# An RWKV/HGRN mixer layer: blockwise transposes by way of DRAM, and a planner's clock for SyncE's queue

## The chip, the cores and the metric

One core of a Trainium2 chip runs the kernel. The metric is the device time of one execution in microseconds; the time before is the median of three runs. Engines are named as the profile names them: PE (TensorE matmul), PEld (its weight loads), DVE (VectorE), ACT (ScalarE), POOL (GpSimd), SP (SyncE, which here only issues DMAs).

## The reference, cut to what matters

One layer over 512 frames and 2048 channels: one input projection, two groups of heads, one output projection, a LayerNorm.

```python
proj = einsum('btd,dc->btc', h, w_in)                 # 512 x 2048 x 8320
rw   = token_shift(proj[..., :RWKV_COLS], shift_mu)   # r, k, v, z and the two low ranks
o    = rwkv7_scan(r, decay, k, v, -kk, kk * a)        # 16 heads of 64, S: 64 x 64 each
o    = (o - mu) * rsqrt(var + GN_EPS) * gn_w + gn_b   # per head
o    = o + sum(r * k * r_k) * v
o_rwkv = o * silu(z)
o_hgrn = rmsnorm(hgrn2_chunkwise(q, f, k, i)) * g_norm_w * silu(z_h)   # 8 heads of 128
y    = einsum('btc,cd->btd', concat([o_rwkv, o_hgrn]), w_out)
out  = layer_norm(ALPHA * x + y, ln_w, ln_b)
```

## The kernel before

**Main stream.** All projections are float32 made of three fp32r products (high x high, high x low, low x high), by the helper `three`; this is PE's main stream, 3900 matmuls. Weights come as `wr` tiles of 512 KB over SP's queue (two buffers); ACT makes the high part `wh` of each half, DVE the low part `wl` (three buffers each). The input projection runs unit by unit in the order of `_order()`. The output projection comes last, in four quarters of 512 columns. A quarter of the first kind has 16 steps of 12 matmuls; a step takes one 128-channel tile of the gated result, split into `xh` (ACT) and `xl` (DVE), against one weight part `wh`, `wl`. At the start of each step `ahead` has the tile of the next step split and reloads tiles that were spilled; in step 8 of the first quarter (steps count from 0) it also sends the DMA of the LayerNorm weights, `big<-ln_wb`, 2 MB. The last four steps use HGRN head 6, RWKV pair 6, HGRN head 7 and RWKV pair 7.

**Side work.** RWKV's 16 heads go as 8 pairs of 128 channels, two pairs to a group. `rwkv_prep` makes a pair's chunked operands: `ar` and `bk` (beta and k times the inverse decay, 8 chunks of 128 columns), scores, and `zz`, which holds v transposed. `rwkv_invert` inverts the chunks' triangular matrices, `rwkv_scan` goes through 8 chunks for two pairs in step, `outputs` adds the part within chunks, and `rwkv_finish` normalizes a pair's result (frames on partitions), turns it back to channels on partitions and gates it.

**The planner.** All engines run in the order in which the Python code issues instructions. `Plan` holds a clock for each engine and a ready and a busy time for each tile, by fixed costs. After every main matmul `pump` goes through queues of generators and issues what its clocks take to be ready: PE work no earlier than 0.35 us after its operands (`LEAD`), other engines' work when it can start within 0.6 us, or its operands come within 0.5 us. `fetched` gives the ready time of a loaded tile: a DMA clock, 360 GB/s and 2 us.

**Transposes before.** `turned` transposes `bk` and v in 32 x 32 blocks on DVE (`dtr`) and then moves the blocks with DMAs from SBUF to SBUF, 32 KB each in runs of 128 bytes: 16 for `bk`, 8 for v. `rwkv_finish` turns its result on PE instead: four `tr` into one PSUM bank, read from there by DVE.

Of the kernel before, what the change touches and what calls it, by code (L numbers as in the profile page):

```python
# [7 lines left out]
F32 = mybir.dt.float32  # L8
# [54 lines left out]
class Plan:  # L63
# [15 lines left out]
    def __init__(self, room):  # L79
        self.clock = {"pe": 0.0, "dve": 0.0, "act": 0.0, "pool": 0.0, "dma": 0.0}  # L80
# [161 lines left out]
def mixer_kernel(ctx, tc, head, x_r, w_all, par, up, ln_wb, consts, hmask, out):  # L242
# [64 lines left out]


# [83 lines left out]
    def turned(dst, src, tmp, rows=4, base=0):  # L392


        name = dst.tensor.name
        yield dtr(tmp, src)
        yield lambda: by_now(tmp)
        for a in range(4):
            for b in range(rows):
                o = base + 32 * b  # L400
                nc.sync.dma_start(dst[o : o + 32, :, 32 * a : 32 * a + 32],
                                  tmp[32 * a : 32 * a + 32, :, 32 * b : 32 * b + 32])
            at = plan.clock["pe"] + 0.4 * rows
            yield lambda: plan.clock["pe"] >= at
        plan.ready[name] = (plan.clock["pe"] + 3.0, "dma")
# [21 lines left out]
    def load(j):  # L427
        if j < nload:
            raws[j] = st("wr", [P, HALF])
            nc.sync.dma_start(raws[j], w_all[j - nhead])  # L430
            plan.fetched(raws[j], 4 * HALF)
# [116 lines left out]
    def constants():  # L548
        raw = st("ksq", [P, T])[:, : 16 * len(LEVELS)]
        for t, a in ((pr, par), (cst, consts), (raw, hmask)):  # L550
            nc.sync.dma_start(t, a)
# [48 lines left out]
    def put_gated(k, g):  # L600

        gated[k] = g
        if k in SPILL:
            def run():
                yield lambda: by_now(g)
                nc.sync.dma_start(spill[SPILL.index(k)], g)
# [8 lines left out]
    def next_up():  # L615
        if len(ups) < NPAIR:
            upw = take("up", [P, 2, P])
            nc.sync.dma_start(upw, up[len(ups)])
# [3 lines left out]
    hc = [slice(64 * h, 64 * h + 64) for h in range(2)]  # L622

    def rwkv_prep(S, p):
# [98 lines left out]
        yield from turned(bk, bk, tmp)  # L723
        drop(tmp)
# [15 lines left out]
        z = take("zz", [P, NCH, P])  # L740
        yield room(ksq=1)
        tmp = take("ksq")
        yield from turned(z, chunks(v), chunks(tmp), rows=2, base=64)
# [3 lines left out]
    def from_v(SS, sc):  # L747
# [6 lines left out]
        for half, (z, ps) in enumerate(zip(zs, pss)):  # L754
            for c in range(NCH):
                for h in range(2):
                    yield mm(ps[hc[h], c * C : c * C + C], sc[64:128, 0, half * 16 + 2 * c + h],
                             z[64:128, c, hc[h]])

        def keep():  # L760
            for z, ps in zip(zs, pss):
                for h in range(2):
                    yield copy(z[0:64, :, hc[h]], chunks(ps[hc[h]]))
# [4 lines left out]
    def outputs(SS, sc):  # L768
# [3 lines left out]
        for half, (S, po) in enumerate(zip(SS, pss)):  # L772
            z = S["zz"]
            yield lambda z=z: by_now(z)
            for c in range(0, NCH, 2):
                for h in range(2):
                    for e in range(2):
                        yield mm(po[hc[e], c // 2 * P + 64 * h : c // 2 * P + 64 * h + 64],
                                 sc[:, 1, half * 16 + 2 * (c + e) + h], z[:, c + e, hc[h]])
# [52 lines left out]
    def rwkv_scan(SS, sc):  # L832
# [11 lines left out]

        for rt, bds, o in zip(rts, bdss, os):
# [5 lines left out]
        for c in range(NCH):  # L851
            more = c < NCH - 1
            zs = [zz[:, c] for zz in zzs]
            news = [bds[c % 2] for bds in bdss]
            pxs = []
            if c > 0:
# [5 lines left out]
                for rt, px, z in zip(rts, pxs, zs):  # L862
                    yield stt(rt[0:64], px[0:64, :P], -1.0, z[0:64], ALU.mult, ALU.subtract)
# [803 lines left out]
```

## Time and profile before

| | |
|---|---|
| Runs | 1050.54 us median of 3 (1049.99 to 1050.96) |
| The profiled execution | 1050.24 us; span 1048.5 us, granted TensorE clock 0.999 |
| DVE, ACT busy | 72% and 42% of the span |
| DMA packets | 87305, of these 56368 under 512 bytes |
| `q<-q` and `zz<-ksq` (blocks moved by `turned`) | 128 and 64 issues of 32 KB |
| Output projection | from 849.7 us on |

The page gives busy times and, in its fourth part, the chain of work that ended last; the timeline gives the start of each instruction, from which PE's real pace is read, since the recorded durations of its matmuls overlap.

### The profile page before, as it was taken

The numbers are of one execution on the slowest core, as the hardware profiler recorded it, in microseconds if no ns is written. First come the engines' busy times: TensorE is split into PE (matmuls) and PEld (weight loads), VectorE is DVE, ScalarE is ACT, GpSimd is POOL, SyncE is SP. The second block draws the span as 40 slices with busy tenths as digits, with TensorE's granted clock in tenths as the row PEclk, the third lists the DMA queues.
The fourth block names the chain that finished last, engine by engine and source line by source line (L and its number), as shares of the span: only waits on it lengthen the run. The fifth ranks groups of instructions, "written<-read, shape, count | busy, mean of one in ns | idle before, by whom it ended". The sixth has DMA issues, their size and how long they took to land.

```text
span 1048.5 us, 18840 instructions
## 1 busy us (share of the span) xinstructions
PE 1040.6 (99%) x7342; PEld 865.1 (83%) x7342; DVE 755.7 (72%) x1653; ACT 437.6 (42%) x867; POOL 38.3 (4%) x81
## 2 busy tenths in 40 slices
PE   9999999999999999999999999999999999999997
PEld 8888888888888888888888888888888888888885
DVE  7465898667759987676689866865998778625556
ACT  6545333445353354452533353525334554323321
POOL 0000000000000000000000000000000002000000
PEclk9999999999999999999999999999999999999999
DMA  8134342222343522223534323234352244545613
GB/s 332 54 103 114 99 109 86 86 79 81 84 123 100 122 82 74 78 98 79 138 78 118 98 62 96 70 96 110 100 128 72 69 164 131 182 131 159 202 60 131
DMA packets 87305, 114.79 MB, mean 109 GB/s; under 512 B 56368, under 2 KB 58160, under 8 KB 87088
## 3 DMA queue, kind: packets, MB, share of 16 engines
q1 hardware_dynamic: 87072, 113.39, 36.6%
q8 instruction: 58, 0.95, 0.4%
q14 instruction: 31, 0.25, 0.1%
q10 hardware_dynamic: 144, 0.20, 0.1%
HBM read 99.92 MB, written 7.34 MB: 102 GB/s over the span
## 4 chain that ended last, share of the span: by engine, by line
PE 99%; DVE 1%; DVEq 0%; issue 0%
PE main L453 74%; PE mix L324 11%; PE mix L453 8%; PE main L1192 3%; PE main L324 2%; PE mix L328 1%; PE mix L1142 0%; DVE inv L356 0%; DVE inv L347 0%; DVE stats L1549 0%; DVEq L1663 0%; DVE mv L1357 0%; DVE bd L356 0%; DVE mv L352 0%; DVE inv L1140 0%
## 5 line engine op out<-in xcount | busy, mean ns | idle before, releaser
L453 PE MATMUL main<-xl,wh 128*128 128x512 f32 x864 | 341.1, 395 | 0.0
L453 PE MATMUL main<-xh,wl 128*128 128x512 f32 x864 | 341.1, 395 | 0.0
L453 PE MATMUL main<-xh,wh 128*128 128x512 f32 x864 | 340.9, 395 | 0.0
L337 ACT ACTIVATE wh<-wr 128x512 fp32r<-128x512 f32 x299 | 186.9, 627 | 237.1 <-PE main L453 180.5
L347 DVE TENSOR_TENSOR wl<-wr,wh 128x512 fp32r<-128x512 f32 x299 | 203.8, 682 | 61.8 <-ACT wh L337 60.1
L453 PEld LDWEIGHTS main<-xh,wh 128*128 128x128 f32 x864 | 162.4, 188 | 33.0
L453 PEld LDWEIGHTS main<-xh,wl 128*128 128x128 f32 x864 | 162.5, 188 | 32.6
L453 PEld LDWEIGHTS main<-xl,wh 128*128 128x128 f32 x864 | 162.4, 188 | 32.6
L453 PE MATMUL main<-wl,xh 128*128 128x512 f32 (+1 forms) x262 | 102.6, 392 | 0.0
L453 PE MATMUL main<-wh,xh 128*128 128x512 f32 (+1 forms) x262 | 102.1, 390 | 0.0
L453 PE MATMUL main<-wh,xl 128*128 128x512 f32 (+1 forms) x262 | 101.6, 388 | 0.0
L453 PEld LDWEIGHTS main<-wh,xh 128*128 128x128 f32 x262 | 49.2, 188 | 9.9
L453 PEld LDWEIGHTS main<-wh,xl 128*128 128x128 f32 x262 | 49.2, 188 | 9.7
L453 PEld LDWEIGHTS main<-wl,xh 128*128 128x128 f32 x262 | 49.2, 188 | 9.6
L338 ACT ACTIVATE t<-main,om 128x512 f32<-128x512 f32 x33 | 22.4, 687 | 51.1 <-PE main L453 41.6
L356 DVE SCALAR_TENSOR_TENSOR t<-main,pr,t 128x511 f32<-128x511 f32 x33 | 24.4, 747 | 26.5 <-ACT t L338 26.2
L347 DVE TENSOR_TENSOR inv<-inv,inv 64x30 f32<-64x30 f32 (+14 forms) x120 | 38.6, 322 | 2.9
L347 DVE TENSOR_TENSOR inv<-inv 64x30 f32<-64x30 f32 (+14 forms) x120 | 38.4, 320 | 2.3
L347 DVE TENSOR_TENSOR t<-t,tot 128x256 f32<-128x256 f32 x96 | 37.8, 414 | 1.8 <-PE mix L324 1.7
L356 DVE SCALAR_TENSOR_TENSOR bd<-mix,pc,bd 64x64 f32<-64x64 f32 x112 | 31.7, 283 | 7.5 <-PE mix L324 5.2
L337 ACT ACTIVATE zz<-mix 64x64 f32<-64x64 f32 x63 | 13.8, 220 | 46.9 <-PE mix L324 45.8
L338 ACT ACTIVATE t<-main 128x512 f32<-128x512 f32 x32 | 18.5, 598 | 30.7 <-PE main L453 30.2
(222 smaller groups left out, 1328.0 us busy)
## 6 DMA issues: line engine op xcount, KB each, us to landing
wr<-w_all SPq DMA_DIRECT2D x156, 512.0 KB, 3.6
q<-head SPq DMA_DIRECT2D x15, 448.0 KB, 5.9
q<-q SPq DMA_DIRECT2D x128, 32.0 KB, 2.4
g<-x_r SPq DMA_DIRECT2D x16, 256.0 KB, 3.8
spill<-g SPq DMA_DIRECT2D x12, 256.0 KB, 2.7
out<-q SPq DMA_DIRECT2D x12, 256.0 KB, 2.4
t<-spill SPq DMA_DIRECT2D x10, 256.0 KB, 4.2
zz<-ksq SPq DMA_DIRECT2D x64, 32.0 KB, 2.6
```

The source lines that it names most:

```text
L324: return Op([("pe", cost, lambda: pe.matmul(o, l, r, start=start, stop=stop, **kw))], [l, r], [o], mode="narrow" if narrow else "main" if ...
L328: return Op([("pe", 0.11, lambda: pe.transpose(o, i, ident))], [i], [o])
L337: return "act", cost, lambda: sc_e.activation(o, i, f, scale=scale)
L338: return "act", cost, lambda: sc_e.activation(o, i, f, scale=scale, bias=bias)
L347: return dve_op([a, b], o, lambda: dve.tensor_tensor(o, a, b, f), base=0.16 if o.shape[0] < P and size(o) == C and o.tensor.name in tags e ...
L356: return dve_op([a, b], o, lambda: dve.scalar_tensor_tensor(o, a, s, b, f1, f2), per=0.00113, base=0.085 if o.shape[0] == P else 0.25 if s ...
L453: pe.matmul(ps, l, r, start=first and i == 0, stop=last and i == 2)
L1192: pe.matmul(pss[a], *ops, start=k == 0 and low == of == 0, stop=k == KT - 1 and low == 1)
```

## The change

`turned` now sends the result of the block transpose to DRAM in one DMA (`far`, 1024 or 512 columns for each partition) and reads it back in one DMA for each 32 rows of the result (four for `bk`, two for v, four for a pair's end), in runs of 1 KB or 512 bytes. The result stands by blocks of 32 columns; for `bk` ACT copies it into the order of chunks, in a `q4` tile that takes `bk`'s place; `zz` keeps the order of blocks, and its readers index it so. `rwkv_finish` turns its normalized result by the same way in place of the four PE transposes; ACT then applies the scale and the bias, and two products on DVE follow. A group's two ends have a queue each. `send` issues every DMA of SP and moves a new clock of the planner, 0.44 us an issue; the ready times of loads start from it, with 1.8 us in place of 2.

```diff
@@ Plan
-        self.clock["dma"] = max(self.clock["dma"], self.clock["pe"]) + size * 128 / 360e3
-        self.ready[tile.tensor.name] = (self.clock["dma"] + 2.0, "dma")
+        self.clock["dma"] = max(self.clock["dma"], self.clock["sp"]) + size * 128 / 360e3
+        self.ready[tile.tensor.name] = (self.clock["dma"] + 1.8, "dma")
@@ helpers
+    def send(o, i):
+        nc.sync.dma_start(o, i)
+        plan.clock["sp"] = max(plan.clock["sp"], plan.clock["pe"]) + 0.44
-    def turned(dst, src, tmp, rows=4, base=0):
-        name = dst.tensor.name
-        yield dtr(tmp, src)
-        yield lambda: by_now(tmp)
-        for a in range(4):
-            for b in range(rows):
-                o = base + 32 * b
-                nc.sync.dma_start(dst[o : o + 32, :, 32 * a : 32 * a + 32],
-                                  tmp[32 * a : 32 * a + 32, :, 32 * b : 32 * b + 32])
-            at = plan.clock["pe"] + 0.4 * rows
-            yield lambda: plan.clock["pe"] >= at
-        plan.ready[name] = (plan.clock["pe"] + 3.0, "dma")
+    def turned(dst, src, tmp, base=0):
+        c = src.shape[1]
+        n = src.shape[2] // 32
+        yield dtr(tmp, src.rearrange("p c (b f) -> p b c f", f=32))
+        yield lambda: by_now(tmp)
+        far = dpool.tile([4, 32, n, c * 32], F32, tag=nm("far"), name=nm("far"))
+        yield lambda: plan.clock["sp"] <= plan.clock["pe"]
+        send(far.rearrange("a p b r -> (a p) b r"), tmp.rearrange("p b c f -> p b (c f)"))
+        at = plan.clock["sp"] + 3.7
+        plan.busy[tmp.tensor.name] = (at, "dma")
+        yield lambda: plan.clock["pe"] >= at
+        for b in range(n):
+            yield lambda: plan.clock["sp"] <= plan.clock["pe"]
+            o = base + 32 * b
+            send(dst[o : o + 32].rearrange("p a c f -> p a (c f)"), far[:, :, b].rearrange("a p r -> p a r"))
+        plan.ready[dst.tensor.name] = plan.busy[dst.tensor.name] = (plan.clock["sp"] + 3.5, "dma")
@@ rwkv_prep
-        yield from turned(bk, bk, tmp)
-        drop(tmp)
+        flat = bk.rearrange("p c t -> p (c t)")
+        yield from turned(blocks(flat, NCH), bk, blocks(tmp.rearrange("p c t -> p (c t)"), NCH))
+        yield copy(tmp.rearrange("p c (a f) -> p a c f", f=32), blocks(flat, NCH))
+        drop(bk)
+        S["bk"] = tmp
-        z = take("zz", [P, NCH, P])
+        z = take("zz", [P, 4, NCH, 32])
@@ rwkv_finish
-        yield room(g=1, ksq=1)
+        yield room(g=1)
         g = take("g")
+        yield from turned(blocks(S["ot"], 4), o_all, blocks(g, 4))
+        yield room(ksq=1)
         sz = take("ksq")
         z = S["z"]
-        yield landed(o_all)
-        po = take("mix")
-        for j in range(4):
-            yield tr(po[:, j * P : j * P + P], o_all[:, j])
         yield act(sz, z, AF.Tanh, scale=0.5)
-        yield stt(g, po, hcol(HGW, p), S["bv"], ALU.mult, ALU.add)
-        drop(po)
+        yield act(in_blocks(g), blocks(S["ot"], 4).rearrange("p a c f -> p c a f"), AF.Identity,
+                  scale=hcol(HGW, p), bias=hcol(HGB, p))
         yield stt(z, sz, 1.0, z, ALU.add, ALU.mult)
-        yield stt(g, g, hcol(HGB, p), z, ALU.add, ALU.mult)
+        yield tt(g, g, S["bv"], ALU.add)
+        yield tt(g, g, z)
@@ rwkv_group
-                plan.add(finishes, rwkv_finish(S, 2 * grp + i))
+                plan.add(finishes[i], rwkv_finish(S, 2 * grp + i))
```

PE, the end of step 10 and the start of step 11 of the output projection's first quarter, before: `xh1487` and `xh1493` are the tiles of these steps, and `t1222` is the normalized result of pair 7.

```order
L453 MATMUL main1416_8955<-wl1486_9296,xh1487_9307 128x512
L453 MATMUL main1416_8955<-wh1485_9295,xl1488_9308 128x512
L453 MATMUL main1407_8896<-wh1489_9318,xh1493_9338 128x512
L328 MATMUL mix1502_9368<-cst_100,t1222_7607 128x128 x4
L453 MATMUL main1407_8896<-wl1490_9319,xh1493_9338 128x512
```

Now (`xh1530` and `xh1535` are the tiles of steps 10 and 11):

```order
L470 MATMUL main1463_8914<-wl1527_9215,xh1530_9234 128x512
L470 MATMUL main1463_8914<-wh1526_9214,xl1531_9235 128x512
L470 MATMUL main1455_8891<-wh1532_9244,xh1535_9258 128x512
L470 MATMUL main1455_8891<-wl1533_9245,xh1535_9258 128x512
L470 MATMUL main1455_8891<-wh1532_9244,xl1536_9259 128x512
```

The four transposes of a pair's end are gone, here as in the other seven pairs; in the whole program small work interrupts the main stream 161 times before and 147 times now, not counting the warm-up and the last four products.

SP, steps 6 to 11 of the same quarter, before (`wr` are weights, `spill` the reloaded tiles, `x_r` the residual):

```order
L430 DMA wr1464_9199<-w_all 128x1024
L1255 DMA t1465_9209<-spill_109 128x512
L430 DMA wr1481_9273<-w_all 128x1024
L1473 DMA big1484_9283<-ln_wb 128x4096
L430 DMA wr1491_9323<-w_all 128x1024
L1456 DMA g1501_9365<-x_r 128x512
```

Now (`t1151` is the result of pair 6, `t1243` that of pair 7):

```order
L310 DMA wr1507_9138<-w_all 128x1024
L310 DMA t1508_9144<-spill_109 128x512
L310 DMA far1512_9153<-g1501_9116 128x512
L310 DMA wr1520_9193<-w_all 128x1024
L310 DMA t1151_6979<-far1512_9153 32x4x128
L310 DMA big1523_9202<-ln_wb 128x4096
L310 DMA t1151_6979<-far1512_9153 32x4x128 x3
L310 DMA far1525_9209<-g1517_9180 128x512
L310 DMA wr1534_9249<-w_all 128x1024
L310 DMA t1243_7468<-far1525_9209 32x4x128 x4
L310 DMA g1542_9290<-x_r 128x512
```

Both pairs' trips now lie around the load of the LayerNorm weights, which comes between the first and the other three reads of pair 6.

ACT, steps 8 to 11, before (`ksq1478` and `ksq1496` belong to pair 7, one normalizing, one gating):

```order
L338 ACTIVATE ksq1478_9265<-t1222_7607 128x512
L337 ACTIVATE xh1487_9307<-t1459_9179 128x512
L337 ACTIVATE wh1489_9318<-wr1464_9199 128x512
L337 ACTIVATE xh1493_9338<-t1465_9209 128x512
L337 ACTIVATE wh1497_9351<-wr1481_9273 128x512
```

Now:

```order
L342 ACTIVATE xh1530_9234<-t1502_9118 128x512
L342 ACTIVATE wh1532_9244<-wr1507_9138 128x512
L343 ACTIVATE g1501_9116<-t1151_6979,half_106 128x512
L342 ACTIVATE xh1535_9258<-t1508_9144 128x512
L342 ACTIVATE wh1537_9271<-wr1520_9193 128x512
```

ACT's scaled copy of pair 6's turned result stands ahead of the split of step 11's tile.

More of the change, by code (lines that the diff above doesn't have):

```diff
@@ L79, in __init__ @@
     def __init__(self, room):
-        self.clock = {"pe": 0.0, "dve": 0.0, "act": 0.0, "pool": 0.0, "dma": 0.0}
+        self.clock = {"pe": 0.0, "dve": 0.0, "act": 0.0, "pool": 0.0, "sp": 0.0, "dma": 0.0}
         self.table = None
@@ L429, in load @@
             raws[j] = st("wr", [P, HALF])
-            nc.sync.dma_start(raws[j], w_all[j - nhead])
+            send(raws[j], w_all[j - nhead])
             plan.fetched(raws[j], 4 * HALF)
@@ L605, in run @@
                 yield lambda: by_now(g)
-                nc.sync.dma_start(spill[SPILL.index(k)], g)
+                send(spill[SPILL.index(k)], g)
                 drop(g)
@@ L622, in mixer_kernel @@
     hc = [slice(64 * h, 64 * h + 64) for h in range(2)]
+    hb = [slice(2 * h, 2 * h + 2) for h in range(2)]
     def rwkv_prep(S, p):
@@ L739, in rwkv_prep @@
         yield room(zz=1)
-        z = take("zz", [P, NCH, P])
+        z = take("zz", [P, 4, NCH, 32])
         yield room(ksq=1)
         tmp = take("ksq")
-        yield from turned(z, chunks(v), chunks(tmp), rows=2, base=64)
+        yield from turned(z, chunks(v), blocks(tmp, NCH), base=64)
         drop(v, tmp)
@@ L762, in keep @@
                 for h in range(2):
-                    yield copy(z[0:64, :, hc[h]], chunks(ps[hc[h]]))
+                    yield copy(z[0:64, hb[h]], ps[hc[h]].rearrange("p (c a f) -> p a c f", c=NCH, f=32))
                 drop(ps)
@@ L852, in rwkv_scan @@
             more = c < NCH - 1
-            zs = [zz[:, c] for zz in zzs]
+            zs = [zz[:, :, c] for zz in zzs]
             news = [bds[c % 2] for bds in bdss]
@@ L868, in rwkv_scan @@
                 for rt, z in zip(rts, zs):
-                    yield copy(rt[0:64], z[0:64], scale=-1.0)
+                    yield copy(by32(rt[0:64]), z[0:64], scale=-1.0)
             yield landed(*rts)
@@ L877, in rwkv_scan @@
                 for h in range(2):
-                    yield copy(z[0:64, hc[h]], block(psa, h))
+                    yield copy(z[0:64, hb[h]], by32(block(psa, h)))
                 drop(psa)
@@ L1254, in reload @@
                 gated[k] = take("t" if plan.free("t") else "g")
[L1255 removed]
+                send(gated[k], spill[SPILL.index(k)])
                 plan.fetched(gated[k], 4 * T)
```

31 lines of the change are left out of this document (18 added, 13 removed).

## The prediction

> **What bounds the kernel now.** I read first the page's busy time and the chain of work that ended last, to learn which engine sets the time:
>
> ```profile
> span 1048.5 us, 18840 instructions
> PE 1040.6 (99%) x7342; PEld 865.1 (83%) x7342; DVE 755.7 (72%) x1653; ACT 437.6 (42%) x867; POOL 38.3 (4%) x81
> PE 99%; DVE 1%; DVEq 0%; issue 0%
> PE main L453 74%; PE mix L324 11%; PE mix L453 8%; PE main L1192 3%; PE main L324 2%; PE mix L328 1%; PE mix L1142 0%; DVE inv L356 0%; DVE inv L347 0%; DVE stats L1549 0%; DVEq L1663 0%; DVE mv L1357 0%; DVE bd L356 0%; DVE mv L352 0%; DVE inv L1140 0%
> ```
>
> The chain is TensorE from end to end, so time can come only from two places: work taken off PE, or waits of PE that appear or go. Everything on DVE, ACT and SP is free as long as PE does not wait for it. Since a busy PE is not a dense PE, I then took the pace from starts. The chain in order of time has a stretch without interruptions, and the timeline shows what an interruption costs (columns: start, duration, engine, line, operation):
>
> ```profile
> 345.51 31.33 PE main L453 x138
> ...
> 703.64 0.39 PE L453 MATMUL main<-xh,wl 128*128 128x512 f32 x1
> 703.88 0.60 PE L328 MATMUL mix<-cst,t 128*128 128x128 f32 x4
> 704.23 0.48 PE L453 MATMUL main<-xh,wh 128*128 128x512 f32 x1
> ...
> 706.63 0.39 PE L453 MATMUL main<-xl,wh 128*128 128x512 f32 x1
> ...
> 447.25 0.39 PE L453 MATMUL main<-xh,wh 128*128 128x512 f32 x1
> 447.48 0.60 PE L324 MATMUL mix<-ia,t 128*128 128x128 f32 x4
> ...
> 448.96 0.48 PE L453 MATMUL main<-xl,wh 128*128 128x512 f32 x1
> ...
> 451.13 0.39 PE L453 MATMUL main<-xl,wh 128*128 128x512 f32 x1
> ```
>
> 31.33/138 = 0.227 us for a main matmul. Between 703.64 and 706.63 there start eleven of them and four transposes: 2.99 - 11 x 0.227 = 0.49 us for four. Between 447.25 and 451.13 there are ten and fourteen small ones (one interruption): 3.88 - 10 x 0.227 = 1.61 us. The difference gives (1.61 - 0.49)/10 = 0.112 us for each instruction of this size, and 0.49 - 4 x 0.112 = 0.04 us for going away from the main stream and back.
>
> **Term 1: what leaves PE.** The pairs' ends lose their four transposes each, 8 x 4 = 32 of the 88 in this group (the other 56 are HGRN's and stay):
>
> ```profile
> L328 PE MATMUL mix<-cst,t 128*128 128x128 f32 x88 | 12.9, 273 | 0.0
> ```
>
> 32 x 0.112 = 3.6 us. In the built order the main stream is interrupted 161 times before and 147 times after (warm-up and the very last products left out), since the planner also puts more small work side by side: 14 x 0.04 = 0.6 us, somewhat more where narrow products are joined. All other PE work is the same in number. Sum: 4.2 us off PE, between 3.6 (nothing for the joints) and 4.8 (twice that).
>
> **What comes in elsewhere, at no cost while PE covers it.** DVE and ACT rows:
>
> ```profile
> L366 DVE STREAM_TRANSPOSE ksq<-t 128x512 f32<-128x512 f32 x8 | 5.6, 701 | 0.0
> L356 DVE SCALAR_TENSOR_TENSOR g<-mix,half,t 128x512 f32<-128x512 f32 x16 | 12.0, 747 | 9.0 <-PE mix L328 8.8
> L347 DVE TENSOR_TENSOR wl<-wr,wh 128x512 fp32r<-128x512 f32 x299 | 203.8, 682 | 61.8 <-ACT wh L337 60.1 <-issue 0.2
> L338 ACT ACTIVATE t<-mix,half 128x512 f32<-128x512 f32 x16 | 10.5, 686 | 16.1 <-PE mix L324 16.1
> L337 ACT ACTIVATE wh<-wr 128x512 fp32r<-128x512 f32 x299 | 186.9, 627 | 237.1 <-PE main L453 180.5 <-PE mix L453 32.9 <-DMA wr<-w_all 13.4
> L337 ACT ACTIVATE xh<-t 128x512 fp32r<-128x512 f32 x10 | 6.2, 619 | 2.8 <-DMA t<-spill 2.8
> ```
>
> Each pair's end gets a DVE transpose of 512 columns (0.70 us) and two products (0.68 each) for two stt (0.75 each): +0.6 us, 8 pairs, 5 us on DVE. ACT gets one scaled copy (0.69) and the copy of bk, 1024 columns, at most 2 x 0.63: 8 x 1.95 = 16 us on an engine that is 42% busy, and its largest idle is waiting for PE (180.5 us in the wh row). The cover is the three wh and wl buffers; if it is gone, each microsecond that ACT is late is one of PE. The reads of zz by PE are now in pieces of 32 columns; no row has just this, so 0 to 1 us, and I take 0, since each piece is still contiguous.
>
> The queue of SP:
>
> ```profile
> wr<-w_all SPq DMA_DIRECT2D x156, 512.0 KB, 3.6
> q<-q SPq DMA_DIRECT2D x128, 32.0 KB, 2.4
> zz<-ksq SPq DMA_DIRECT2D x64, 32.0 KB, 2.6
> spill<-g SPq DMA_DIRECT2D x12, 256.0 KB, 2.7
> up<-up SPq DMA_DIRECT2D x8, 128.0 KB, 3.2
> big<-ln_wb SPq DMA_DIRECT2D x1, 2048.0 KB, 10.1
> ```
>
> 192 issues become 24 writes and 80 reads; weight loads have less ahead of them on SP. A turn is now two trips. The planner allows 0.44 + 3.7 us for the write (nearest: 2.7 for 256 KB; 512 KB somewhat more) and 3.5 us after the last read is sent (nearest: 3.2 for 128 KB). So where only a weight load lies in the way, the allowance holds and ACT, which now waits for data of a DMA in 16 places (8 bk copies, 8 ends), waits little. I put 0 there, at most 16 x 0.5 = 8 us.
>
> **Term 2: the end of pair 6 meets the 2 MB load.** In one place the allowance cannot hold. In the new order SP sends, in the ninth step (step 8, from 0) of the output projection's first quarter, `big<-ln_wb`, and the last three of the four reads of pair 6's turned result stand behind it; in ACT's order the scaled copy of that result (g<-t) stands ahead of `xh` of step 11 (both are shown in the section on the change). The same place before:
>
> ```profile
> 883.99 0.69 DVE L347 TENSOR_TENSOR wl<-wr,wh 128x512 fp32r<-128x512 f32 x1
> 884.35 0.39 PE L453 MATMUL main<-wh,xh 128*128 128x512 f32 x1
> 884.70 0.33 SPq L430 DMA_DIRECT2D wr<-w_all  x1
> 885.13 1.26 SPq L1473 DMA_DIRECT2D big<-ln_wb  x1
> 890.09 0.33 SPq L430 DMA_DIRECT2D wr<-w_all  x1
> 896.54 0.63 ACT L337 ACTIVATE wh<-wr 128x512 fp32r<-128x512 f32 x1 [2.21 <-DMA wr<-w_all]
> ```
>
> PE starts step 8 at 884.35 (call it P), big is sent at P+0.8. The weight load sent five microseconds later is seen by ACT only at 896.54, 6.4 us after its issue and 11.4 after big's: what is behind big comes after big. So the reads are complete 10.1 to 11.4 us after big is sent (its own landing, and that of the load behind it); 192 KB are less than that load's 512, so I take 10.5. Big itself is sent after a weight load that waits for step 9's wl. In the new order no interruption slows steps 6 and 7, and step 9's wh needs only the end of step 6, at P-2.7: wh 0.63, wl 0.68 and 0.3 of handing over end at P-1.1, with two issues big goes at P-0.4; if DVE is as busy as before, at P+0.8 and 0.4 for the extra read, P+1.2. I take P+0.2. The result is there at P+10.7 (P+9.7 to P+12.6). Then ACT does g (0.69) and xh (0.62), DVE xl (0.68), with 0.1 for the handing over: P+12.8. PE wants step 11 after 36 main matmuls and one group of four transposes, P + 36 x 0.227 + 0.46 = P+8.6, and xl two matmuls later, at P+9.1. PE stands 3.7 us, between 2.7 and 5.6. I take 3.6, a little below, since DVE has less to do there than before. Pair 7's write and reads come behind the same load, but its result is wanted only in step 15, after PE's own stop, so I add nothing.
>
> **Term 3: the clock after such a stop.** Stretches at the kernel's end, cut back in steps of 3.4 us from the place where the clock changes (columns: busy time and count by engine, then PE's granted clock):
>
> ```profile
> 1038.90:1042.30 3.40, 1.88 (x5) 0.68 (x4) 3.30 (x10) 0.40 (x1) 0.54 (x1) 1.00 0.00 0
> 1042.30:1045.70 3.40, 1.24 (x3) 0.19 (x1) 2.15 (x5) 0.00 (x0) 0.00 (x0) 1.00 0.77 260
> 1045.80:1048.40 2.60, 0.00 (x0) 0.00 (x0) 0.00 (x0) 0.00 (x0) 0.00 (x0) 0.50 0.19 53
> ```
>
> With PE busy 1.88 of 3.4 us the clock stayed full; after 1.24 of 3.4 it was 0.50. A stop of 3.6 us leaves one such stretch with at most 1.6 busy, wherever it falls, so I expect the drop in some three of four runs of the kernel, and it costs half of PE's work in about one stretch less what is left of the stop: 0 to 1.7 us, I take 1.2. The Trainium skill ("TensorE: Matmul & The Clock Gate", Part 1) says that the array falls to half rate after at least one idle window of 3.4 us that runs free of the kernel. Taken by its word, a 3.6 us stop would rarely hold a whole window and term 3 would be near 0, for a time of 1049.8; this trace shows the drop after a stretch that was a third busy, so the row decides.
>
> **The sum.** 1050.24 us is the profiled execution's own time; its span is 1048.5, with 1.7 us around it; the median of the runs is 0.3 above it, at 1050.54. -4.2 + 3.6 + 1.2 = +0.6: 1050.8 by the profiled execution, 1051.1 by the median. I forecast 1051.0, no change that a measurement can tell: 0.2% is 2.1 us, about what a measurement of this kernel can tell from none.
>
> **Rivals.** (a) The reads are not held up: the rings let them pass, or ACT's order costs nothing. Then only term 1 counts: 1050.5 - 4.2 = 1046.3, faster. For it: 192 KB is little, and the load at 890.09 overlaps big's last packets. Against it: that load came 2.8 us later than the 3.6 us that the page gives for its kind. It decides if the result lands before P+7.0, that is 6.8 us after big is sent. The Trainium skill ("DMA: Bandwidth & Descriptors", Anatomy of one DMA) fits a transfer as 2.0 us plus bytes over 436 GB/s. By that, as an estimate, big would be done in 6.8 us where the row has 10.1, the stop would vanish and the time be 1046.3; the measured row decides against it. (b) Slower: ACT's 16 waits for turned data are not covered in the scan stages, where products wait for copies of ACT; PE then stands in each for what the data is late beyond three wh buffers. With 0.5 us in half of them this adds 4 us: 1055. It decides when reads land later than 3.5 us after sending; against it stand 2.4 to 3.2 us in the rows above. (c) The stop is at its long end, 5.6 us, and the clock costs 1.7: -4.2 + 7.3 = +3.1, 1053.6, slower.
>
> **How the numbers follow.** The case of terms 1 to 3 has 70%, by its bounds from 1049.0 (-4.2 + 2.7) to 1053.6; I see 52 of these within 0.2% of 1050.5 (1048.4 to 1052.6), 16 above it (rival c) and 2 below. Rival (a) has 18%, all faster. Rival (b) has 12%: 2 within, 10 slower. So faster 0.20, same 0.54, slower 0.26. The range reaches from (a), 1046.2, to 1053.6, and leaves out most of (b) and the ends of (a).
>
> **What would show it.** Right: 56 transposes at the line of 328; PE's interruptions fewer by 14; one idle stretch of PE of some 3 us near 890, in which ACT's g<-t is released by the DMA from `far` and PE by xh or xl; a granted clock of 0.5 for some 3 us behind it; no other PE wait above 0.5 us. Wrong: no PE idle there with the reads landing in under 7 us (then 1046), or idle of PE spread over the four scan stages, ahead of it ACT's copies waiting for `far` (then 1055).

## The result, and the profile after

| | before | after |
|---|---|---|
| Median | 1050.53 us | 1060.28 us (1059.41 to 1064.16, four executions) |
| Ratio | | 1.0100, interval 1.0081 to 1.0119 |
| The profiled execution | span 1048.5 us, clock 0.999 | 1064.16 us, span 1062.4 us, clock 0.991 |

The changed kernel is 1% slower; the forecast was 1051.0, at most 1053.6. From the page after (span, busy time, chain by engine):

```profile
span 1062.4 us, 18727 instructions
...
PE 1044.6 (98%) x7310; PEld 867.5 (82%) x7310; DVE 758.8 (71%) x1657; ACT 449.8 (42%) x887; POOL 39.6 (4%) x81
...
PE 90%; DMA 4%; DVE 3%; ACT 1%; issue 1%; SPq 0%; POOL 0%; DVEq 0%; ACTq 0%
```

The chain was PE to 99%; now 10% of it is others' work. What PE waited for (total, times, longest, in us):

```profile
PE main L470 <- ACT xh L342: 6.1, 1, 6.1
PE mix L329 <- issue: 1.6, 1, 1.6
PE mix L329 <- ACT ksq L1432: 1.5, 1, 1.5
PE main L329 <- issue: 1.4, 1, 1.4
PE mix L1165 <- DVE inv L1163: 1.1, 1, 1.1
PE mix L329 <- ACT zz L342: 0.7, 1, 0.7
```

Before, PE's list had three rows:

```profile
PE mix L324 <- ACT ksq L1409: 1.5, 1, 1.5
PE mix L1142 <- DVE inv L1140: 1.1, 1, 1.1
PE mix L324 <- DVE bd L356: 0.4, 1, 0.4
```

The rows of `ksq` at 1432 and of `inv` belong to the kernel's end and start and are as before. The first row is the stop that term 2 foretold. The two rows of "issue", in which PE waited for nothing that the profile shows, were not foretold, and neither was the 0.7 us for `zz`. The timeline at the tail (start, duration, engine, line, operation, idle time before and its releaser):

```profile
890.37 0.37 SPq L310 DMA_DIRECT2D t<-far  x1
...
890.78 0.42 SPq L310 DMA_DIRECT2D big<-ln_wb  x1
...
891.26 1.42 SPq L310 DMA_DIRECT2D t<-far  x3
...
903.08 0.81 ACT L343 ACTIVATE g<-t,half 128x512 f32<-128x512 f32 x1 [9.94 <-DMA wr<-w_all]
...
903.80 0.61 ACT L342 ACTIVATE xh<-t 128x512 fp32r<-128x512 f32 x1
...
904.44 0.69 DVE L352 TENSOR_TENSOR xl<-t,xh 128x512 fp32r<-128x512 f32 x1 [8.95 <-ACT xh L342]
```

The three reads behind the 2 MB landed 10.7 to 11.1 us after their issue; ACT stood 9.94 us, `xh` of step 11 behind it, and PE with it. (The row names a weight load as releaser, but none landed then: by the trace the last of the three reads landed at 902.93, the weight loads sent nearest to it at 893.82 and 904.48.) The windows of 3.41 us in which the granted clock changes (busy time and count by engine, then the clock):

```profile
182.37:185.78 3.41, 1.86 (x70) 1.53 (x67) 1.52 (x4) 0.79 (x3) 0.00 (x0) 1.00 0.03 10
185.79:189.19 3.40, 3.40 (x9) 2.63 (x8) 2.77 (x9) 2.33 (x6) 0.00 (x0) 0.50 0.02 5
605.63:609.03 3.40, 2.02 (x110) 1.85 (x100) 0.61 (x4) 1.18 (x2) 0.00 (x0) 1.00 0.54 158
609.05:612.45 3.40, 3.40 (x91) 3.02 (x90) 1.80 (x4) 0.94 (x3) 0.00 (x0) 0.50 0.02 6
612.46:615.86 3.40, 3.40 (x10) 2.63 (x9) 3.06 (x11) 1.79 (x5) 0.00 (x0) 0.50 0.00 0
899.18:902.58 3.40, 0.00 (x0) 0.00 (x0) 0.00 (x0) 0.00 (x0) 0.00 (x0) 1.00 0.90 290
902.60:906.00 3.40, 1.54 (x4) 1.20 (x5) 1.56 (x3) 2.92 (x6) 0.00 (x0) 0.50 0.30 98
```

The clock fell to half in three places, not one. At half clock a main matmul starts every 0.427 us instead of 0.227, which the starts show for 27 of them: 5.4 us.

I accounted for each interruption of the main stream as its time above 0.227 us per main matmul, less what the same small instructions cost elsewhere in the two traces (0.111 us for one of 128 x 128, 0.04 for the interruption). Span after minus before, 13.9 us, is then, but for 0.1:

| | us |
|---|---|
| 32 transposes and 14 interruptions less | -4.1 |
| Step 11: stop 6.2, `xl` behind it 0.4, half clock and the rest | +9.1 |
| Joined narrow runs near 183 and 607: stops and half clock | +3.2 +4.1 |
| Small waits near 333, 446 and 760 | +0.4 +1.0 +0.9 |
| A wait near 845 that is gone | -0.6 |

### The profile page after: what moved, and what is told of

Read it like the earlier page. It is cut to its first block, busy times and chain, and to the rows that moved or that the text cites. A ratio compares the mean times of both kernels' runs of the same rounds, so it can differ in the third digit from the quotient of the medians.

```text
span 1062.4 us, 18727 instructions
## 1 busy us (share of the span) xinstructions
PE 1044.6 (98%) x7310; PEld 867.5 (82%) x7310; DVE 758.8 (71%) x1657; ACT 449.8 (42%) x887; POOL 39.6 (4%) x81
## 4 chain that ended last, share of the span: by engine, by line
PE 90%; DMA 4%; DVE 3%; ACT 1%; issue 1%; SPq 0%; POOL 0%; DVEq 0%; ACTq 0%
PE main L470 66%; PE mix L329 10%; PE mix L470 8%; PE main L1215 3%; DMA wr<-w_all 3%; PE main L329 2%; DMA q<-far 1%; DVE wl L352 1%; DVE inv L371 1%; PE mix L333 1%; PE mix L1165 0%; DVE inv L361 0%; DVE t L352 0%; SPq L310 0%; ACT L343 0%
## 5 line engine op out<-in xcount | busy, mean ns | idle before, releaser
L470 PEld LDWEIGHTS main<-wl,xh 128*128 128x128 f32 x262 | 49.8, 190 | 10.7 <-DVE wl L352 0.5
L470 PEld LDWEIGHTS main<-wh,xl 128*128 128x128 f32 x262 | 49.8, 190 | 10.4 <-DVE xl L352 0.2
L342 ACT ACTIVATE zz<-mix 64x64 f32<-64x64 f32 x78 | 17.0, 218 | 38.8 <-PE mix L329 38.0
```

What stands on the lines that cost most here:

```text
L342: return "act", cost, lambda: sc_e.activation(o, i, f, scale=scale)
L470: pe.matmul(ps, l, r, start=first and i == 0, stop=last and i == 2)
```

## Experiments

Theory A: the tail stop comes from the 2 MB ahead of pair 6's reads. C: the stops in the joined runs come from the fetch of PE's instructions. D, the rival: DRAM trips and their traffic cost by themselves. E and F came up on the way. Times are set against the kernel before on the same chip (1050.4 to 1050.7 us).

### The stop at the tail

`late_ln`: the 2 MB behind the last reads.

```diff
-            if j == 8:
+            if j == 13:
```

> The changed kernel with the load of ln_wb moved from step 8 to step 13 of the output product, behind the last reads of pair 7. Theory A (the 6.2 us stop at step 11 is the queue of pair 6's reads behind the 2 MB): those reads land some 2.3 us after their issue, the stop at step 11 goes, and with it the half clock behind it (10 mains at 427 instead of 227 ns, 2.0 us): 1060.3 - 6.6 - 2.0 = 1051.7 us, between 1050.5 and 1053. The two stops of 1.6 to 1.8 us in the joined runs of narrow matmuls (near 183 and 607) stay, each with a half clock behind it. Rival B (the DRAM trip of the last pairs is too long in any case): a stop of 3 us or more stays at step 11 or 13, 1056 to 1060.

Measured 1054.27 us (1051.4 to 1058.6), ratio 1.0040 (1.0025 to 1.0054), above the range of the forecast. The tail's four reads landed 3.4 to 4.1 us after their issue, and no wait for `xh` is left among PE's:

```profile
PE mix L329 <- issue: 1.5, 1, 1.5
...
PE main L329 <- issue: 0.7, 1, 0.7
PE mix L329 <- ACT zz L342: 0.7, 1, 0.7
```

So A holds for the tail: one number moved gives back 6.0 us by the medians. Against the profiled execution of the changed kernel the span is 9.9 us shorter: 6.6 us are the stop and the wait for `xl`, 3.2 the half clock (2.2 us of it here against 5.4). The sum was 2.6 too low.

`half_ln`: 1 MB at step 8 and 1 MB at step 13.

> The changed kernel with ln_wb loaded in two halves of 1 MB, one at step 8 as before, the other at step 13: a dose of the same cause. Theory A: in the changed kernel the three reads landed 10.7 to 11.1 us after their issue against 2.3 elsewhere, so the 2 MB held them up for 8.6 us; 1 MB holds them up for about 4.3, the stop of 6.6 shrinks to 6.6 - 4.3 = 2.3 us (1.5 to 3), with or without a half clock behind it (0 to 2.0): 1060.3 - 4.3 - (0 to 2.0) = 1054.0 to 1056.0. Rival B (length of the trip, not the 2 MB): unchanged, 1059 to 1061.

Measured 1059.75 us, ratio 1.0096 (1.0079 to 1.0113). The reads landed 8.2 to 8.8 us after their issue, between 3.4 to 4.1 with nothing and 10.7 to 11.1 with 2 MB ahead, and PE's stop is

```profile
PE main L470 <- ACT xh L342: 3.5, 1, 3.5
```

The order A gives is right, the proportion is not: half the bytes leave more than half of the delay. The median is outside A's range (1054 to 1056) and inside B's (1059 to 1061), although the stop and the delay of the reads say A. Half clock followed the shorter stop too, and the medians hold different amounts of it: against the profiled execution of the changed kernel the span is 5.6 us shorter, 2.6 by the stop and 2.6 by the clock.

### The joined runs: instruction fetch and clock

In the changed plan HGRN's 64 narrow products (`mix<-t` and `mix<-t,t`) and RWKV's 64 (`main<-zz,big` and `mix<-inv,big`) stand side by side in two places, 512 PE instructions (weight loads and two passes counted) without a main matmul; before, the longest run had 264. The page has a DMA queue for instructions:

```profile
q8 instruction: 57, 0.93, 0.4%
```

57 packets of 16 KB against 14,620 instructions of PE and PEld: 256 a packet. Counted in order, with PE's 162 semaphore instructions among them, both stops begin 192 instructions past a multiple of 256. In quiet stretches a packet starts when PE is some 80 to 105 short of such a multiple. So, as an estimate, about 298 instructions are at hand when a fetch is due; where they pass before it ends, PE stands.

`doses` puts this into the kernel before, which has no DRAM trip, by issuing narrow matmuls again:

```diff
+                for n in range((3, 0, 2, 1)[grp] * 32):   # after the 32x32 products; group 1: 3 x 32 of the 64x64 ones
+                    pe.matmul(pq[32 * g : 32 * g + 32, j], l, r, start=True, stop=True)
```

> The kernel before, without any turning by way of DRAM, in which some narrow matmuls of the RWKV groups are issued again (the same operands into the same place, 96 times the 32x32 ones in group 0, 96 times the 64x64 ones in group 1, 64 times the 32x32 ones in group 2, 32 times in group 3), the plan untouched; the added work takes 1.9 + 6.7 + 1.3 + 0.6 = 10.5 us by the paces in the trace (10 ns a pass of a 32x32, 35 ns of a 64x64). Theory C (instruction fetch): the stop depends on how fast 298 instructions from the point of the fetch pass. Group 0: 1.55 us, so a stop of 2.3 to 3.3 us at an instruction 193 past a multiple of 256; group 1, although it is as many instructions, 4.0 us, so 0 to 0.9; group 2: 3.1 us, 0.7 to 1.8; group 3: 2.9 us, 1.0 to 2.0; half clock behind the first at least. 1050.5 + 10.5 + 4 to 8 + clock 2 to 6 = 1067 to 1075. Rival D (the stops come from the DRAM traffic of the turned data): no stop without a releaser in any of the runs, 1061.

Measured 1070.61 us, once, inside the range. The stops are there, without a DRAM trip:

```profile
185.08 0.78 PE L828 MATMUL mix<-inv,big 32*32 32x32 f32 x39
187.09 1.13 PE L828 MATMUL mix<-inv,big 32*32 32x32 f32 x64 [1.23 <-issue]
```

Four steps between PE starts, of 1.46 us (group 0), 0.71 and 0.60 (group 1) and 0.29 (group 3), all begin at instruction 192 past a multiple of 256, as do the two each of `late_ln` and `half_ln`. In these, as in both profiles of the changed kernel, PE goes on 1.2 to 1.5 us after the last packet of the instruction queue is through. C is shown, D falls for these stops. Their sizes were foretold too large, and the one of group 2 did not come: with its stop, the stretch of 298 took 3.6 us in group 0 (3.1 to 5.0 in all of these kernels). The surprise was the clock behind group 2, where PE had no stop over 0.3 us:

```profile
619.36:622.76 3.40, 3.40 (x203) 3.23 (x198) 2.53 (x7) 0.74 (x2) 0.00 (x0) 1.00 0.38 141
622.78:626.18 3.40, 3.40 (x9) 2.65 (x8) 0.69 (x1) 1.93 (x5) 0.00 (x0) 0.50 0.02 5
```

Half clock after a window in which PE was busy throughout, with narrow matmuls. Hence theory F, that the clock goes by how much of the array works and not by whether PE is busy, and `clock_area`, again in the kernel before:

```diff
+                n = (32, 64, 128, 0)[grp]
+                for _ in range(40 if n else 0):
+                    pe.matmul(pt[0:n], xh[0][0:n, 0:n], xh[0][0:n], start=True, stop=True)
```

> The kernel before, in which three of the RWKV groups get 40 added matmuls without any wait or gap, 512 columns each (227 ns, 9.1 us a block), into a bank that is written over afterwards: on 32 rows by 32 columns of the array in group 0 (near 183 us), 64 by 64 in group 1 (near 380), 128 by 128 in group 2 (near 625). Theory F (the granted clock goes by how much of the array worked in a window of 3.41 us, not by whether PE was busy): half clock within or behind the block of 32 by 32 (a sixteenth of the array), none at 128 by 128; 64 by 64 (a quarter) lies at the edge, since windows with 0.17 to 0.23 of the array's work stayed at full clock in these traces and such with 0.07 to 0.15 did not. Rival G (only idle time counts): full clock in all three, 1050.5 + 27.2 = 1077.7 us. By F 2 to 6 us more.

Measured 1087.25 us, once. The blocks of 32 x 32, of 64 x 64 and of 128 x 128:

```profile
181.48:184.88 3.40, 3.40 (x68) 2.43 (x63) 2.35 (x5) 1.59 (x3) 0.00 (x0) 1.00 0.52 153
184.90:188.30 3.40, 3.40 (x10) 1.31 (x8) 0.89 (x5) 0.00 (x0) 0.00 (x0) 0.50 0.00 0
...
191.72:195.12 3.40, 3.40 (x9) 1.31 (x8) 0.00 (x0) 0.00 (x0) 0.00 (x0) 0.50 0.00 0
...
387.93:391.33 3.40, 3.40 (x17) 2.82 (x16) 3.35 (x4) 1.09 (x2) 0.00 (x0) 1.00 0.00 0
...
637.50:640.90 3.40, 3.40 (x16) 2.82 (x16) 0.00 (x0) 0.00 (x0) 0.00 (x0) 1.00 0.00 0
```

With PE busy in every window, the clock went to half and stayed there for 20.5 us (to 205.4) with a sixteenth of the array at work, and stayed full with a quarter and with all. G falls, and F holds for these blocks; where between a sixteenth and a quarter the edge lies was not measured, nor whether rows, columns or their product count. `apart`, below, shows that F is not the whole rule. 9.6 us were lost against the 1077.7 of full clock; "2 to 6" was too little, since the block itself runs at half rate.

`after_2` is the changed kernel again, unchanged.

> The changed kernel once more, for a second profile. The profiled execution had 1064.16 us, the other three 1059.4 to 1060.7. Theory: the stops are the same (6.2 at step 11, 1.6 to 1.8 in the two joined runs, within 0.7), and the difference lies in how many windows of half clock follow them, which depends on where the 3.4 us windows fall: one window less is 1.5 to 2.0 us less. 1058.5 to 1061 where three windows are granted half, 1062 to 1064 where five are. Rival: other waits differ between executions.

Measured 1065.40 us (1062.6 to 1066.9), ratio 1.0132 (1.0117 to 1.0148). The stops are the same (5.7, 1.4 and 1.3 us by the list of waits), but each of the three places has two windows at half clock here, six where the forecast had at most five, and the time is above its range. Over both sets of executions, time goes with the granted clock: 0.997 with 1059.4 and 1059.8, 0.995 with 1060.7 and 1062.6, 0.992 and 0.991 with 1064.7 and 1064.2, 0.989 with 1066.2 and 1066.9. Carried on to the 0.999 of the kernel before, at 0.86 us for each 0.001, that is some 1058: about 7 us of the loss are stops and waits net of the gain, and 2 to 9 us, by where the windows fall, are clock.

### One part alone

`sp_only`: the kernel before with `send` and the planner's clock for SP.

> The kernel before with the planner's clock for SyncE's queue alone (0.44 us for each issue, loads taken as started by it, 1.8 instead of 2.0 us to land), the turning by 32x32 DMAs and PE transposes as before. The plan has 163 interruptions against 161, no run over 264 instructions. Theory A: 1050.4 + 2 x 0.04 = 1050.5, between 1049.8 and 1051.2. Rival (the new clock makes the joined runs and the late ends): 1053 or more.

Measured 1050.49 us, ratio 0.9998 (0.9989 to 1.0007). The clock of the planner by itself changes the time by no more than 0.1% either way.

`ends_pe`: pairs' ends by PE transposes, beta, k and v by DRAM. `HOLD` is the time in us for which the planner holds back narrow products that are ready, so that others can join them; 0.8 in place of 1.0 leaves no run of 512 (the longest has 384).

> The changed kernel with the ends of the pairs turned by PE transposes as in the kernel before, beta-and-k and v by way of DRAM, HOLD at 0.8, ln_wb at step 8. Theory A: no pair's end is behind the 2 MB any more, so no tail stop; the 32 transposes are back (32 x 0.111 = 3.6 us) and there are 159 interruptions against 161: 1050.5 - 0.1, with 0 to 1 us for small waits on turned data: 1050.0 to 1051.5. Rival D (beta, k and v by way of DRAM cost by themselves): 1053 or more.

Measured 1055.95 us, ratio 1.0047 (1.0032 to 1.0062), at full clock. A's sum failed; D's number came out. The timeline shows how:

```profile
489.52 0.95 SPq L310 DMA_DIRECT2D q<-far  x2
...
495.65 1.06 ACT L342 ACTIVATE q<-q 128x1024 f32<-128x1024 f32 x1 [4.04 <-DMA q<-far]
496.61 0.61 ACT L342 ACTIVATE ksq<-t 128x512 fp32r<-128x512 f32 x1
...
497.28 0.50 PE L329 MATMUL mix<-ksq,ones_r 128*128 128x512 f32 x1 [1.12 <-ACT ksq L342]
```

ACT has its copy of `bk` in its order as soon as the plan has the reads done, 3.5 us after the last is sent; here the last three landed 4.7 to 5.5 us after, and the square that PE wants next stood behind the copy. That is rival (b) of the prediction. Theory E says that only ACT's wait costs, D says the traffic. `ends_pe_pool` has the copy on GpSimd:

```diff
-        yield copy(tmp.rearrange("p c (a f) -> p a c f", f=32), blocks(flat, NCH))
+        yield Op([("pool", 0.1 + size(o_) * 0.003, lambda: pool.tensor_copy(o_, i_))], [i_], [o_])
```

> As the kernel with the ends by PE transposes (1055.95 us), but the copy that takes beta-and-k back from DRAM on GpSimd instead of ScalarE, so that no instruction of ScalarE waits for that DMA. There ACT waited 21.1 us in 6 waits (5.4 at most) for q<-far, and PE stood behind it for squares that ScalarE issues next (1.1 us near 496, some 5 us in all). No run over 264 PE instructions in the plan, 161 interruptions as before. Theory E (the loss there is ScalarE's wait for the reads, which land 4.5 to 5.5 us after their issue where the plan has 3.5): 1055.95 - 5 = 1051, between 1050.0 and 1052.0. Rival D (the DRAM traffic costs by itself): 1054 or more.

Measured 1051.59 us, ratio 1.0009 (1.0000 to 1.0018): 4.4 of the 5.4 us went with ACT's waits, while the traffic stays. E holds; for D at most the rest is left, 0 to 1.9 us by the interval. (The new copy also gives another plan; how much of the 4.4 us that is was not separated.)

`apart`: the changed kernel with `HOLD` 0.8 alone.

```diff
-    HOLD = {"whole": 0.6, "narrow": 1.0}
+    HOLD = {"whole": 0.6, "narrow": 0.8}
```

> The changed kernel with HOLD for narrow matmuls at 0.8 alone: no run of 512 PE instructions, ln_wb still at step 8, now ahead of the trips of both last pairs on SyncE's queue. Theory A with C: no PE stop without a releaser and full clock before the tail; the tail stop stays, 6 to 9 us with 2 us of half clock: 1052.0 - 3.4 + 8 to 11 = 1056.6 to 1059.6. Rival (the joined runs are harmless, the tail stop alone makes the loss): as the changed kernel, 1060.3, with half clock near 183 or 607.

Measured 1053.30 us, ratio 1.0029 (1.0020 to 1.0038): 7.0 us less than the changed kernel, and less than expected, because in this plan the 2 MB goes out ahead of pair 6's write too, and the tail's stop is 1.9 us. No stop without a releaser and no half clock ahead of the tail. So the joined runs are not harmless; but the number also holds another tail, and I don't read it as theirs alone. The window behind which the clock fell, and the next; then the same of a run that comes below, `late_apart`:

```profile
895.11:898.52 3.41, 1.56 (x7) 1.00 (x6) 1.72 (x3) 1.81 (x3) 0.00 (x0) 1.00 0.79 199
898.53:901.93 3.40, 3.40 (x9) 2.43 (x8) 2.84 (x5) 1.70 (x4) 0.00 (x0) 0.50 0.58 180
...
901.12:904.53 3.41, 1.52 (x7) 0.94 (x5) 1.38 (x2) 1.44 (x3) 0.00 (x0) 1.00 0.99 394
904.54:907.94 3.40, 3.35 (x13) 2.47 (x14) 3.33 (x6) 1.04 (x2) 0.00 (x0) 1.00 0.90 314
```

In both, PE stood for some 1.9 us and was busy for some 1.5 with matmuls of 128 x 128, which is more of the array's work than a window of the 64 x 64 blocks has; yet the clock fell in one and not in the other. So F does not account for the clock behind a stop, and what it goes by there stays open.

### What the change is worth without its accidents

`late_apart`: `HOLD` 0.8 and the 2 MB at step 13.

> The changed kernel with the load of ln_wb at step 13 and the planner's HOLD for narrow matmuls at 0.8 instead of 1.0, by which the plan has no run of 512 PE instructions left (longest 384, three pairs of runs in another order). Theory A with C (C: PE runs out of fetched instructions where 298 of them pass in less than 3.8 to 4.9 us; here the shortest such stretch is worked out at 3.65 us): no stop of 6 us at step 11, at most 1.2 us of stop by instructions in all, no half clock or one: 1060.3 - 8.6 - (3.4 + 3.7 for the joined runs) = 1044.6, less what the small stops seen in the changed kernel keep; 1045 to 1049, faster than the kernel before (1050.5). Rival D (the turning by way of DRAM costs by itself, the stops in the joined runs come from its traffic): the stops stay in other places, 1051 to 1056.

Measured 1052.05 us, ratio 1.0016 (1.0007 to 1.0025), above the range. Another wait had taken the place:

```profile
894.30 0.33 SPq L310 DMA_DIRECT2D t<-far  x1
...
897.34 0.33 SPq L310 DMA_DIRECT2D g<-x_r  x1
...
897.72 1.37 SPq L310 DMA_DIRECT2D t<-far  x3
...
901.55 0.82 ACT L343 ACTIVATE g<-t,half 128x512 f32<-128x512 f32 x1 [2.88 <-DMA t<-far]
...
904.59 0.50 PE L470 MATMUL main<-wh,xh 128*128 128x512 f32 x1 [1.95 <-ACT xh L342]
```

Between pair 7's first read and the other three stands a load of `x_r`, which waits 3 us for its buffer; SP stands with it. `best` has `x_r` in steps 13 to 15 and the 2 MB in step 15:

> The changed kernel with HOLD for narrow matmuls at 0.8 (no run of 512), the first slice's loads of x_r at steps 13 to 15 instead of 11 to 14, and ln_wb at step 15, so that on SyncE's queue nothing stands between the reads of pairs 6 and 7. The run with ln_wb at step 13 alone had 1052.0 us; in its trace the load of x_r between pair 7's first read and the other three waited 3 us for its buffer, and PE then stood 2.3 us at step 12, with 3.5 us in all put down to that interruption. Theory A: that goes and nothing takes its place: 1052.0 - 3.4 = 1048.6, between 1047 and 1050, faster than before. Rival D (a DRAM trip costs by itself; the next one late shows instead): 1050.5 or more, with a PE wait of 2 us or more at the tail.

Measured 1049.46 us, ratio 0.9991 (0.9982 to 0.9999), at full clock: inside the range, and ahead of the kernel before, barely. `pool_copy` adds the copy on GpSimd:

> As the best kernel so far (HOLD 0.8, x_r at steps 13 to 15, ln_wb at step 15: 1049.46 us), with that copy on GpSimd instead of ScalarE. Theory E: the stop of 1.0 us near 336, where ScalarE waited 3.4 us for q<-far, goes, with 0.3 to 0.8 us of smaller ones; 151 interruptions: 1049.46 - 1.3 = 1048.2, between 1047.0 and 1049.2. One stop of 0.1 to 0.5 us by instructions (298 of them in 3.49 us near 607) is in this. Rival (ScalarE's wait costs nothing at the end, or GpSimd's copy is late and takes its place): 1049.4 or more.

Measured 1049.22 us, ratio 0.9990 (0.9982 to 0.9999). That is at the edge of its range, and no difference from `best` that these runs can tell. In its profiled execution (1047.58 us, the lowest) ACT's stop near 336 is gone. The others went up to 1051.24. Six of the eleven had a clock of 0.997 or 0.998, and the plan has a run of 352 narrow instructions, which would fit F; but the slowest had 0.999, so this spread stays open. `reads_55` leaves the copy on ACT and gives the plan 5.5 us for these reads:

> As the best kernel so far, but with HOLD at 1.0 again and the plan's time for the reads of beta and k at 5.5 us after their issue instead of 3.5 (they landed 4.5 to 5.5 after it), ScalarE still making the copy, which the plan now issues later; no run of PE instructions over 264. Theory E: as the GpSimd copy, 1049.46 - 1.0 = 1048.5, between 1047.5 and 1049.5. Rival (a later plan gives the time back in the scan stages, since beta and k come 2 us later): 1050 or more.

Measured 1049.00 us, ratio 0.9985 (0.9976 to 0.9994), inside the range. PE has a stop of "issue" here too, though no run is over 264:

```profile
PE mix L329 <- issue: 1.0, 1, 1.0
```

It lies at the same place of the count and ends 1.4 us after a packet, but the 298 instructions took 7.1 us; `last_pe_55` and `ends_pe` have one each of 0.5 and 0.3 us, after 6.6 and 10.6 us. What made these packets late isn't shown. `best_2` was to have the copy on GpSimd and no run over 272, by 4.2 us for a DRAM write:

> As the kernel with the copy on GpSimd (1049.22 us; in 6 of its 11 executions the clock was 0.997 or 0.998, and its plan has a run of 352 narrow instructions near 607), with the planner's wait for a DRAM write at 4.2 us instead of 3.7, by which the plan has no run over 272 and the ends of the last pairs stay early; 157 interruptions instead of 151 (+0.25). Theory A with C and F: full clock in all executions but for the end, 1050.65 - 3.9 + 0.25 + 0.5 = 1047.5, between 1046.8 and 1048.8. Rival (other waits take the gain): 1049 or more.

Measured 1051.53 us, ratio 1.0009 (0.9999 to 1.0018): the rival. In this plan ACT's g<-t waits for pair 7's reads with a weight part `wh` behind it, and PE stands 1.5 us for that part's `wl`. `last_pe` and `last_pe_55` therefore turn the last two pairs' ends on PE as before:

> The changed kernel with the ends of the last two pairs alone turned by PE as in the kernel before (8 transposes), the other six by way of DRAM, the copy of beta and k on GpSimd, HOLD at 0.6; ln_wb and x_r where the changed kernel has them. No PE run over 272 instructions, 158 interruptions. Theory A with C, E and F: 24 transposes x 0.111 + 3 x 0.04 = 2.8 us gained, no DRAM trip left at the tail: 1050.7 - 2.8 = 1047.9, between 1047.3 and 1049.2, clock 0.999 or 1.000. Rival (the gain of the transposes is not there, and other waits always take it): 1050 or more.

> The same split of the ends, ScalarE making the copy, with the plan's time for the reads of beta and k at 5.5 us and HOLD at 1.0; no PE run over 272, 153 interruptions. Theory: 24 x 0.111 + 8 x 0.04 = 3.0 us gained, 0.5 to 1.5 us of waits of the kernel with these reads (1049.0 us, 1.1 us near 815 among them) kept: 1048.5, between 1047.7 and 1049.5. Rival: 1050 or more.

`last_pe`: 1053.07 us, ratio 1.0022 (1.0013 to 1.0031). A miss again, of one kind with the others but at an earlier pair, with the reads 5.6 to 6.2 us on their way, behind reads of `bk` and a weight load:

```profile
287.73 1.79 SPq L310 DMA_DIRECT2D t<-far  x4
...
294.83 0.82 ACT L343 ACTIVATE g<-t,half 128x512 f32<-128x512 f32 x1 [5.86 <-DMA t<-far]
...
296.74 0.49 PE L329 MATMUL mix<-ksq,ones_r 128*128 128x512 f32 x1 [1.18 <-ACT ksq L342]
```

`last_pe_55`: 1048.67 us, ratio 0.9981 (0.9972 to 0.9990), the fastest of all. Its page:

```profile
span 1046.3 us, 18738 instructions
...
PE 1038.0 (99%) x7318; PEld 863.6 (83%) x7318; DVE 755.8 (72%) x1657; ACT 451.8 (43%) x885; POOL 40.0 (4%) x81
...
PE 97%; DVE 2%; issue 0%; POOL 0%; ACT 0%; DVEq 0%; ACTq 0%
```

By the accounting above it has 2.9 us less small PE work and interruptions than before and 0.8 more of waits; 1.9 us are measured. So the gain of term 1 exists, and two thirds of what this version could have are seen; the 0.8 us are 0.5 of "issue" and 0.3 for DVE.

## Why the prediction was wrong, point by point

The forecast was 9.3 us too low. Two of its steps failed. It put the joints of narrow work at a gain and no PE wait outside the tail above 0.5 us: the two joined runs cost 3.2 and 4.1 us, by instruction fetch and half clock. And it put terms 2 and 3 at 4.8 us: they came to 9.1. Term 1's gain of 4 us is there by the accounting and is outweighed.

- **Term 1** (-4.2): right in size by the accounting (-4.1). What failed is the 0.6 in it for joints. That the planner "puts more small work side by side" was booked as a gain of 0.04 us each; two of these joints cost 3.2 and 4.1 us. The order had shown both, and I looked at their number and not at their length.
- **"At no cost while PE covers it"**, with ACT's waits at 0: the 3.5 us allowance, put beside 3.2 us for 128 KB loads, was too short: the reads of `bk` have a median of 3.5, so half are late, and up to 4.6 where a weight load stands ahead (5.5 in `ends_pe`, with a spill there too). In the changed plan it cost 1.3 us, near 333 and 760, where ACT's copy waited; near 446 no DMA is waited for, ACT had two table loads of 1.28 us ahead of `zz`. In `ends_pe`, another plan, 4.4 of 5.4 went with ACT's waits. The mechanism of rival (b) was right; where it strikes, and for how much, is up to the plan.
- **Term 2**: right in place and cause; the size was off, 6.2 + 0.4 against 3.6 (2.7 to 5.6). P was 889.58; big went at P+1.2, the upper end of its range (P+0.2 taken), and the last of the reads landed 12.2 us after big was sent, against 10.5 taken and 11.4 at most. The bound came from the one weight load sent behind big in the trace of before; the load of `x_r` sent next there landed 12.0 us after big was sent and would have given a wider one. Here big itself took 11.3 us instead of 10.1.
- **Term 3** (1.2, one drop): the step that failed is that the clock falls only behind a window in which PE was idle for about half of the time or more, so only at the tail. Half clock came in three places, for one or two windows each: 5.4 us in the profiled execution. Behind 1.86 and 2.02 us busy of 3.41 it fell, where the prediction's row with 1.88 had kept it. The Trainium skill ("TensorE: Matmul & The Clock Gate", Part 1) lets the clock go by how busy PE has been; `clock_area` shows half clock with PE busy throughout, so the runs decide. Its other statement, that the window is free-running, so that the same kernel meets it at different phases, agrees: the first rise to full clock came 4.88 us after the start of the span in one profile of the changed kernel and 7.24 in the other, and the times spread from 1059.4 to 1066.9.
- **"No other PE wait above 0.5 us"**: wrong three times, at 1.6, 1.4 and 0.7 us; the instruction fetch was not in the list of things that PE can wait for.
- The rivals: (a) fell: the result landed 12.2 us after big was sent, against its 6.8. The fit that it quotes from the Trainium skill ("DMA: Bandwidth & Descriptors", Anatomy of one DMA) is given there for transfers issued by GpSimd; these go by SyncE's queue, where big took 10.1 and 11.3 us. Of (b) see above; (c) had the right sign and a third of the size.

## What to carry to other kernels

Where a transpose goes by DRAM, ask which in-order engine waits for the trip and what stands behind that wait on it; a large load or a load that waits for a buffer, put between the reads on the same queue, made PE stand for 6 and 2 us here. The planner's time for such a trip must be that of a loaded queue. When a planner puts narrow matmuls side by side, look at the length of the run: a few hundred instructions of some ten nanoseconds can outrun their fetch (the two joined runs of 512 did in all four profiles that have them, and 256 in three others), and a window of 3.4 us filled with 32 x 32 tiles brings the half clock, also without any wait.

## What the runs showed of the hardware that I had not expected

- PE's instructions come in packets of 16 KB, 256 instructions (57 packets for 14,620 rows). Where some 298 of them would pass before the next packet, PE stood until 1.2 to 1.5 us after it (1.78 us at most), and the profile names no releaser ("issue"); with its stop, such a stretch took 3.1 to 5.0 us. In three runs it took 6.6 to 10.6; why is open.
- A busy PE does not keep the clock: it was granted half with PE busy throughout on 32 x 32 tiles, and full on 64 x 64 and 128 x 128. Behind stops of 1.9 us it fell once and stayed once. It falls and rises in steps of 3.41 us that begin at another phase in each profile.
- The reads of 64 KB sent behind a 2 MB load on the same queue landed 10.4 to 11.1 us after their issue (two profiles), behind 1 MB 8.2 to 8.8, behind none 3.4 to 4.1.
